# A two-layer decoder trunk on one core: residual stream kept feature-major, output projection with stationary weights, both norms folded

## The chip, the cores and the metric

The kernel runs on one core of a Trainium2 chip. The time is device microseconds of one execution. Before the change the median of three runs is 699.74 us (699.06 to 700.9).

## The reference, cut to what matters

512 prompt tokens and 8 × 4 = 32 sample tokens share the weights of two layers (D = 1024). All arrays are float32.

```python
def _rmsnorm(x, w):
    return x * lax.rsqrt(jnp.mean(x * x, axis=-1, keepdims=True) + EPS) * w

def _layer(x, ...):
    h = _rmsnorm(x, norm_w)
    z = h @ w_in                       # 1024 x 3584
    rq, rk, rv, rg, mq, mk, mv, mg, pu, pg = jnp.split(z, _split_points(), axis=-1)
    r_o = retention(rope(rq), rope(rk), rv)         # 6 heads x 64
    m_o = block_sparse_attention(rope(rmsnorm(mq)), rope(rmsnorm(mk)), mv)
    p_o = pooling(pu)                               # windows 2, 4, 8, 16
    mix = concat([r_o * silu(rg), m_o * silu(mg), p_o * silu(pg)])
    return x + mix @ w_out             # 1024 x 1024

for l in range(2):
    xp = _layer(xp, ...)   # 512 prompt tokens
    xs = _layer(xs, ...)   # 32 sample tokens, with caches and states
```

Besides the two results the new keys, values and states of both layers are outputs.

## The kernel before, in words

**Order.** Every piece of work is a generator that yields `R(engine, keys, get, mode)`: the engine (or a choice such as "ACT|DVE"), the flags it waits for, the buffers it takes, and the shape in which TensorE is used. `_Plan` (L118) takes the step that can start first by its modelled costs, so the program has one fixed order on each engine; at run time only semaphores delay it. SP issues the transfers, in its own fixed order: weight slices, cache pages, residual loads and stores share it.

**Projections.** A weight chunk ("mv", "mq", ..., "rg", "o0", "o1", "o2"; `order`, L422) is 384 or 256 columns wide and comes in four slices of two 128-row blocks each (`wraw`). ACT rounds a slice to fp32r and DVE (or POOL) subtracts to get the low part, both into `whl` (five buffers). A float32 product is three fp32r passes, hi·hi, lo·hi, hi·lo (`PASSES`), over 8 k-blocks: 24 matmuls for an output piece, which takes one of two PSUM banks "acc". In the token form (`tok_piece`, L474) 128 tokens of `XT` are the stationary operand and 384 or 256 weight columns stream: the trace calls it `acc<-whl,XT`, and its result is token-major. In the feature form (`feat_piece`, L483) 128 weight columns are stationary and the tokens stream, 256 of them for half 0 and 288 for half 1 (256 prompt and the 32 sample tokens): `acc<-XT,whl`, result feature-major. The gates and the pool input (pu, pg, mg, rg) have the feature form. The others, the output projection o0 to o2 among them, have the token form, and there the sample tokens go by a plain float32 product of their own (`sample_piece`, L506: `dec<-wraw,...`, 32 matmuls of half the chunk's width), joined by `join_sample`.

**Layer 0's norm** is folded: `xt` comes from the host feature-major, `split_tokens` multiplies by the norm's weights per feature (`ncol`) and splits into `XT`'s high and low part; `norm_tokens` and `split_sample` sum squares beside that, and `spread_norms` makes the token scales `rs`, and `Rb`, the same scales spread over all partitions. Projections' results are scaled afterwards: token-major ones by `rs` per partition, feature-major ones on DVE, `acc<-acc,Rb` (L1163, L1244).

**Output projection and layer 1's norm.** `split_mix` (L1491) writes the gated mix into `XT` once the last input chunk has been multiplied. `residual` (L1506) loads x in 15 pieces; `post_out` (L1521) adds them, token-major, into `mix` (`ytile`), and for the samples into a t1 buffer. After o2, `rmsnorm(l, t)` (L547) works for each of the four token tiles and the samples: ACT squares and sums, POOL takes the power −0.5, DVE multiplies by scale and weights (`SCALAR_TENSOR_TENSOR qT/kT<-mix,rst,pt`), TensorE transposes eight 128×128 blocks (`tr<-cst,qT`, L352), ACT and DVE write the high and low part into `XT`. In layer 1 the projections need no scale afterwards.

The lines that the steps of the prediction touch:

```python
    def tok_piece(ci, n, t, a, ks, i):
            mm(a[:, :W], XT[:, k, xl, t * 128:(t + 1) * 128], w1 if wl else w0, ...)
    def feat_piece(ci, n, f, half, a, ks, i):
        n0, n1 = (0, 256) if half == 0 else (256, NTOK)
            mm(a[:, :n1 - n0], wt[ci, k // 2][:, wl, c0:c0 + 128], XT[:, k, xl, n0:n1], ...)
```

Of the kernel before, what the change touches and what calls it, by code (L numbers as in the profile page):

```python
# [10 lines left out]
F32 = mybir.dt.float32  # L11
# [33 lines left out]
TOKENS = ["mq", "mv", "mk", "rq", "rv", "rk", "o0", "o1", "o2"]  # L45
# [68 lines left out]
SP_PRIO = 2  # L114
WARM = 1


class _Plan:  # L118
# [8 lines left out]
    SWITCH = 0.1  # L127

# [55 lines left out]
    def _start(self, t):  # L184
        engines, keys, get, mode = t["want"]
# [61 lines left out]
def R(engines, keys=(), get=(), mode=FULL):  # L247
    return engines, tuple(keys), tuple(get), mode
# [61 lines left out]
def trunk(ctx, tc, depth, xp, xt, xs, xst, kv, sret, spool, pt, nrow, ncol, lpar, w384, w256, cst, y0,  # L310
# [64 lines left out]
    def ytile(t, c0=0, W=D):  # L375

        return mix[:, c0 // 128:(c0 + W) // 128, t * 128:(t + 1) * 128]

    def col3(x):
        return x.rearrange("p (k c) -> p k c", c=128)  # L380

# [25 lines left out]
    ncolt = const.tile([128, 8], F32, name="ncol")  # L407
# [84 lines left out]
    def chunk(ci, outs, ks=KS_IN):  # L492

        for oi_, (piece, keys, post) in enumerate(outs):
            for i in range(0, 8, 2):
                s_ = ks[i] // 2
                yield R("PE", [("w", ci, s_)] + ([] if i else list(keys)), [] if i else ["acc"])
# [6 lines left out]
            X.spawn(post(a), 1, X.then())  # L504

    def sample_piece(ci, n, x, keys, post):  # L506
# [4 lines left out]
        yield R("PE", [("raw", ci, s_) for s_ in order_] + list(keys), ["dec"], COLS32)  # L511
# [35 lines left out]
    def rmsnorm(l, t, L):  # L547
        rows = 128 if t < 4 else NS
        tag = ("qT", "qT", "kT", "kT", "PT")[t]
        st = sb([128, 3], "rst", 4)  # L550
        if t == 4:
            yield R("SP", [("ys", l)], ["P", "P"])
            x = [buf("P")[:rows] for _ in range(2)]
            for half in range(2):
                S.dma_start(x[half], y0[SEQ:, :][:, half * 512:half * 512 + 512])
                X.flag("xs", l, at=X.dma(64))
            x = [col3(h) for h in x]
            yield R("ACT", [("xs", l)], [tag, tag])
            xn = [buf(tag)[:rows] for _ in range(2)]
            for half in range(2):  # L560
                A.activation(col3(xn[half]), x[half], AF.Square, accum_out=st[:rows, half:half + 1])
            yield R("POOL")
            G.tensor_tensor(out=st[:rows, 0:1], in0=st[:rows, 0:1], in1=st[:rows, 1:2], op=OP.add)
        else:
            x = ytile(t)
            pair = "xn", t // 2
            yield R("ACT", [("y", l, t)] + [("xn", l, t)] * (t % 2), [] if t % 2 else [tag])
            if t % 2 == 0:
                L[pair] = [buf(tag), 4]
                X.flag("xn", l, t + 1)  # L570
            xn = L[pair][0][:, t % 2 * D:(t % 2 + 1) * D]
            xn3 = col3(xn)
            A.activation(xn3, x, AF.Square, accum_out=st[:, 0:1])
            yield R("POOL")
            x, xn = [x[:, 0:4], x[:, 4:8]], [xn[:, 0:512], xn[:, 512:D]]
        rsq(st[:rows, 2:3], st[:rows, 0:1], 1, rows, 1.0 / D)
        c0 = t * 128

        def turned(half):
            yield R("PE", [("cst0",)], ["tr"], FULL if t < 4 else ROWS32)  # L580
            p = ps("tr")
            for i in range(4):
                tr(p[:, i * rows:(i + 1) * rows], xn[half][:, i * 128:(i + 1) * 128], rows)
            if t == 4:
                X.put(tag)
            else:
                L[pair][1] -= 1
                if not L[pair][1]:
                    X.put(tag)
            pv = p[:, :4 * rows].rearrange("p (k n) -> p k n", k=4)  # L590
            ksl = slice(half * 4, half * 4 + 4)
            yield R("ACT")
            A.copy(XT[:, ksl, 0, c0:c0 + rows], pv)
            if t == 4:
                A.copy(X32[:, ksl, :], pv)
            yield R("DVE")
            V.tensor_tensor(out=XT[:, ksl, 1, c0:c0 + rows], in0=pv,
                            in1=XT[:, ksl, 0, c0:c0 + rows].bitcast(F32), op=OP.subtract)
            X.put("tr")
            X.flag("x", l, t, half)  # L600

        for half in range(2):
            if half == 0 or t == 0:
                yield R("DVE", [("row", l, half)] + ([("row", l, 1)] if t else []))
            V.scalar_tensor_tensor(col3(xn[half]), x[half], st[:rows, 2:3], col3(L["row"][half][:rows]),
                                   op0=OP.mult, op1=OP.mult)
            if t == 4:
                X.put("P")
            X.spawn(turned(half), 0, X.then())
        if t == 4:  # L610
            X.flag("normed", l)

# [20 lines left out]
    def projected(a, dst, t, Ct, St, scale=None, eps=None, norm=None):  # L633
# [25 lines left out]
        if scale is None:  # L659
# [6 lines left out]
            def root():  # L666
                yield R("POOL")
                rsq(st[:rows, 1, :H], st[:rows, 0, :H], H, rows, 1.0 / HD, EPS if eps is None else eps)
                X.flag(*key)
# [132 lines left out]
    def layer(l):  # L802
# [3 lines left out]
        def parameters():  # L806
            yield R("SP", () if l else [("xs issued",)], ["pt"])
            rowp = L["rowp"] = buf("pt")
            if l:
                L["row"] = [rowp[:, :512], rowp[:, 512:D]]  # L810
                S.dma_start(rowp[:, :D], nrow[l:l + 1, :D].to_broadcast([128, D]))
                at = X.dma(512)
                for i in range(2):
                    X.flag("row", l, i, at=at)
                yield R("SP")
            S.dma_start(rowp[:, D:D + 256], nrow[l:l + 1, D:].to_broadcast([128, 256]))
# [3 lines left out]
            yield R("DVE", [("normed", l)] if l else ())  # L820
# [15 lines left out]
        def tables(i):  # L836
# [3 lines left out]
            for j, base in enumerate((cos, sin)):  # L840
                c0 = D + 128 * i + 64 * j
# [135 lines left out]
        def post_mq(t):  # L977
            def f(a):
                yield R("DVE", [("tabs", l, 0)], ["qk"])
                q_ = buf("qk")  # L980
                yield from projected(a, q_, t, L["tabs", 0][:, 0, t], L["tabs", 0][:, 1, t], eps=eps_of(t), norm=norm)
# [25 lines left out]
        def scaled_copy(out, a, t, keys=()):  # L1007

            if l:
                yield R("ACT|DVE", keys)  # L1010
                copy(out(), a)
                return
            yield R("ACT|DVE", [("rs", t // 2), *keys])
# [5 lines left out]
        norm = None if l else rs[:, 1, 4:5]  # L1019

        def eps_of(t):
            return None if l else rs[:128 if t < 4 else NS, 2, t:t + 1]

        def post_mv(t):
            def f(a):
# [4 lines left out]
                if t < 4:  # L1030
                    yield from scaled_copy(lambda: L["tv"][:, t], a[:, :384], t, [("tvb", l)])
# [862 lines left out]
```

## Time and profile before

| | |
|---|---|
| median of three runs | 699.74 us (699.06 to 700.9) |
| the profiled execution | 698.75 us |
| its span, first to last instruction | 697.0 us |
| mean granted clock of TensorE | 1.000 |
| transfers | 159.76 MB, 229 GB/s over the span |

The profile is of one execution. Its span leaves out 1.75 us of that execution's time, and the execution is 1.0 us below the median. Engines are PE (TensorE's products), PEld (its loads of the stationary operand, beside PE), DVE, ACT, POOL and SP (which issues transfers). A row such as `acc<-whl,XT` names what is written and what is read; the line of a row is that of a helper for nearly every operation (L342 products, L352 transposes, L304 everything else), so rows are told apart by their tiles.

### The profile page before, as it was taken

How to read it: one execution, taken by the hardware profiler on the slowest of the kernel's cores; microseconds unless marked ns; L12 is line 12 of the kernel's file. 1: busy time of each engine (PE TensorE's matmuls, PEld its weight loads, DVE VectorE, ACT ScalarE, POOL GpSimd, SP SyncE). 2: the span in 40 equal slices, each digit the busy share in tenths (PEclk: the TensorE clock that was granted, in tenths of full speed). 3: DMA queues.
4: the chain of work that ended last, by engine and by line, in shares of the span. 5: the costliest groups of instructions: out<-in, count | busy, mean ns of one | idle time of the engine just before them, and what ended most of it. 6: DMA issues, size and time to landing. Idle time of an engine off the chain costs nothing.

```text
span 697.0 us, 16955 instructions
## 1 busy us (share of the span) xinstructions
PE 676.4 (97%) x5940; PEld 568.5 (82%) x5940; DVE 489.4 (70%) x1169; ACT 330.6 (47%) x831; POOL 106.8 (15%) x134
## 2 busy tenths in 40 slices
PE   7999999999999999899989999999999999999998
PEld 6997777777788879889978778777687888999998
DVE  6789988785662668975494699775845556877642
ACT  7453765662342334464363437676724234256520
POOL 4332223000000022200021223230100000151000
PEclk9999999999999999999999999999999999999999
DMA  8667978898989886435653887998899996020552
GB/s 314 226 205 231 287 232 274 258 310 291 325 261 296 304 266 210 119 124 174 192 177 129 265 270 246 303 314 288 291 278 293 336 321 227 2 83 20 173 176 79
DMA packets 111366, 159.76 MB, mean 229 GB/s; under 512 B 13937, under 2 KB 96114, under 8 KB 111282
## 3 DMA queue, kind: packets, MB, share of 16 engines
q1 hardware_dynamic: 111010, 158.43, 69.8%
q8 instruction: 47, 0.77, 0.4%
q10 hardware_dynamic: 272, 0.26, 0.2%
q14 instruction: 37, 0.30, 0.1%
HBM read 148.80 MB, written 9.84 MB: 228 GB/s over the span
## 4 chain that ended last, share of the span: by engine, by line
PE 86%; DVE 8%; ACT 2%; issue 2%; DMA 1%; POOL 0%; DVEq 0%; ACTq 0%
PE acc L342 54%; PE pv L342 12%; PE dec L342 10%; PE tr L352 6%; PE att L342 4%; DVE whl L304 2%; DVE XT L304 1%; DMA mix<-xt 1%; ACT whl L304 1%; DVE t L304 1%; DVE acc L304 1%; DVE qk L304 0%; ACT kT L304 0%; DVE kT L304 0%; DMA pk<-kv 0%
## 5 line engine op out<-in xcount | busy, mean ns | idle before, releaser
L342 PE MATMUL acc<-whl,XT 128*128 128x384 f32 (+1 forms) x1680 | 312.6, 338 | 4.7 <-ACT whl L304 3.2
L342 PEld LDWEIGHTS acc<-whl,XT 128*128 128x128 f32 x1680 | 282.2, 190 | 23.8 <-issue 14.0
L342 PE MATMUL acc<-XT,whl 128*128 128x256 f32 (+1 forms) x960 | 139.6, 295 | 4.0 <-DVE t L304 2.4
L342 PEld LDWEIGHTS acc<-XT,whl 128*128 128x128 f32 x960 | 124.7, 189 | 15.0 <-issue 10.4
L304 ACT CAST whl<-wraw 128x768 fp32r<-128x768 f32 (+1 forms) x100 | 77.0, 781 | 48.8 <-PE acc L342 42.8
L304 DVE TENSOR_TENSOR whl<-wraw,whl 128x768 fp32r<-128x768 f32 (+1 forms) x91 | 83.3, 928 | 16.6 <-ACT whl L304 16.0
L342 PE MATMUL dec<-pk,qblk 128*32 128x256 f32 x768 | 48.3, 383 | 0.0
L304 DVE TENSOR_TENSOR pv<-pv,cst 128x384 f32<-128x384 f32 x40 | 22.5, 563 | 28.3 <-PE pv L342 27.8
L342 PEld LDWEIGHTS dec<-pk,qblk 128*32 128x32 f32 x768 | 21.8, 109 | 17.4 <-issue 4.3
L304 DVE TENSOR_TENSOR mix<-acc,qk 128x384 f32<-128x384 f32 (+1 forms) x24 | 12.2, 508 | 24.7 <-PE acc L342 23.8
L304 ACT ACTIVATE P<-att,ast 128x128 f32<-128x128 f32 (+3 forms) x48 | 25.2, 530 | 8.4 <-DVE ast L304 8.2
L304 POOL TENSOR_TENSOR qst<-qst,mhalf 128x6 f32<-128x6 f32 (+1 forms) x20 | 26.5, 1324 | 1.7
L304 POOL TENSOR_TENSOR whl<-wraw,whl 128x768 fp32r<-128x768 f32 (+1 forms) x9 | 17.7, 1971 | 53.7 <-issue 28.5
L304 DVE TENSOR_REDUCE stat<-dec 128x1 f32<-128x256 f32 x32 | 13.5, 421 | 15.4 <-PE dec L342 15.1
L304 ACT ACTIVATE dPT<-dec 128x256 f32<-128x256 f32 x32 | 12.2, 382 | 24.8 <-PE pv L342 24.7
L304 POOL TENSOR_TENSOR gst<-gst,reps 128x6 f32<-128x6 f32 x4 | 0.8, 200 | 150.2 <-DVE gst L304 150.2
L304 ACT ACTIVATE dP<-dec,stat 128x256 f32<-128x256 f32 x32 | 15.1, 473 | 15.8 <-DVE stat L304 15.7
L304 ACT COPY PT<-tr 128x128 f32<-128x128 f32 (+3 forms) x40 | 16.0, 429 | 12.6 <-PE tr L352 12.6
L304 ACT ACTIVATE t<-acc 128x256 f32<-128x256 f32 (+1 forms) x32 | 12.6, 394 | 18.9 <-PE acc L342 10.2
L304 DVE TENSOR_REDUCE ast<-att 128x2 f32<-128x256 f32 (+3 forms) x24 | 19.8, 825 | 0.8
L352 PE MATMUL tr<-cst,P 128*128 128x128 f32 x120 | 19.3, 278 | 0.8 <-DVE so L304 0.6
L304 ACT ACTIVATE PT<-PT,gst 128x64 f32<-128x64 f32 x48 | 16.8, 428 | 6.6 <-POOL gst L304 6.6
(504 smaller groups left out, 1184.8 us busy)
## 6 DMA issues: line engine op xcount, KB each, us to landing
pk<-kv SPq DMA_DIRECT2D x256, 192.0 KB, 3.8
wraw<-w SPq DMA_DIRECT2D x76, 384.0 KB, 4.9
wraw<-w SPq DMA_DIRECT2D x24, 256.0 KB, 4.5
y<-mix SPq DMA_DIRECT2D x4, 512.0 KB, 3.6
mix<-xt SPq DMA_DIRECT2D x7, 256.0 KB, 5.9
pk<-w SPq DMA_DIRECT2D x4, 384.0 KB, 4.9
o_vp<-tv SPq DMA_DIRECT2D x8, 192.0 KB, 2.7
o_kp<-qk SPq DMA_DIRECT2D x8, 192.0 KB, 3.8
```

Of the source, the lines that this page charges most:

```text
L304: return f(*args, **kw)
L342: nc.tensor.matmul(out, lhsT, rhs, start=start, stop=stop)
L352: nc.tensor.transpose(out, in_, ident[:n, :n])
```

## The change

The output projection takes the feature form in both layers, sample tokens included (as columns 256 to 287 of half 1), so the residual stream is feature-major throughout: `mix` holds x + mix @ w_out by features, `xsT` that of the samples, and `y0`, the results and the residual loads have feature-major layouts (16 pieces of 128 KB a layer). `rmsnorm` with its transposes is gone; layer 1 uses layer 0's `split_tokens`, `norm_tokens`, `split_sample` and `spread_norms`, so all its projections are scaled afterwards. The first chunk, mv, goes by halves of the tokens in both layers: half 0 in the "att" banks and half 1 in the "acc" banks, and its bank is copied out before it is scaled. `norm_tokens` squares on ACT and adds on DVE alone. The planner gets two constants for changes of TensorE's shape (STAY, LEAVE).

```diff
-TOKENS = ["mq", "mv", "mk", "rq", "rv", "rk", "o0", "o1", "o2"]
+TOKENS = ["mq", "mv", "mk", "rq", "rv", "rk"]
...
                 if mode != self.mode:
-                    late = self.HOLD if self.mode == FULL else 0.3
+                    late = (hold or self.HOLD) if self.mode == FULL else 0.3
+                elif mode != FULL:
+                    late = self.STAY
                 c = max(at + late, self.free[e])
+            elif e == "PE" and self.mode != FULL:
+                c = s + self.LEAVE
...
-    def rmsnorm(l, t, L):
...
-            x = ytile(t)
...
-            A.activation(xn3, x, AF.Square, accum_out=st[:, 0:1])
...
-                tr(p[:, i * rows:(i + 1) * rows], xn[half][:, i * 128:(i + 1) * 128], rows)
...
         def post_mv(t):
...
-                    yield from scaled_copy(lambda: L["tv"][:, t], a[:, :384], t, [("tvb", l)])
-                    X.put("acc" if l or t < 2 else "att")
+                    yield R("ACT|DVE", [("tvb", l)])
+                    copy(L["tv"][:, t], a[:, :384])
+                    X.put("att" if t < 2 else "acc")
+                    yield from scaled_copy(lambda: L["tv"][:, t], L["tv"][:, t], t)
...
             def f(a):
-                if l == 0:
-                    yield R("DVE", [("Rb",)])
-                    V.tensor_tensor(out=a[:, :n], in0=a[:, :n], in1=Rb[:, n0:n1], op=OP.mult)
+                yield R("DVE", [("Rb", l)])
+                V.tensor_tensor(out=a[:, :n], in0=a[:, :n], in1=Rb[:, n0:n1], op=OP.mult)
...
+        def split_mixs():
+            yield R("ACT|DVE", [("dec", l, g) for g in range(2)] + [("inputs", l, 1)] +
+                    [(n, l, f, 1) for n, m in (("pg", 2), ("rg", 3)) for f in range(m)])
+            copy(XT[:, :, 0, SEQ:], mixs)
+            yield R("DVE")
+            V.tensor_tensor(out=XT[:, :, 1, SEQ:], in0=mixs, in1=XT[:, :, 0, SEQ:].bitcast(F32), op=OP.subtract)
+            X.flag("mixs", l)
...
+        def post_out(h, f):
+            def g(a):
+                yield R("DVE", [("res", l, h, f)])
+                out = mix[:, f, 256 * h:256 * h + 256]
+                V.tensor_tensor(out=out, in0=a[:, :256], in1=L["res", h, f][:, :256], op=OP.add)
+                if h:
+                    V.tensor_tensor(out=xsT[:, f], in0=a[:, 256:256 + NS], in1=xsT[:, f], op=OP.add)
+                X.put("acc")
                 X.put("qk")
...
+                X.flag("xt", l + 1, h, f)
+                send((y0 if l < depth - 1 else o_yp)[h, f // 2][:, f % 2 * 256:f % 2 * 256 + 256], out, 128)
...
             for n in ("o0", "o1", "o2"):
-                yield from tokens(n, lambda t: post_out(n, t), lambda t: [("mix", l, t)], KS_OUT)
+                steps = chunk(c(n), [(feat(n, f, h), mixed(h), post_out(h, fo)) for h, f, fo in out_pieces(n)], KS_OUT, 0)
+                for i, x in enumerate(steps):
+                    yield x
+                    if n == "o2" and i in (7, 15):
+                        X.flag("oh", l, i // 8)
...
-    def split_tokens(h, kp):
+    def split_tokens(l, h, kp):
...
-        yield R("ACT|DVE", [("xt", h, kp), ("ncol",)])
+        yield R("ACT|DVE", [("xt", l, h, k) for k in ks] + ([("oh", l - 1, h)] if l else [("ncol",)]))
...
-    def norm_tokens(h):
...
-            yield R("ACT|POOL", [("xt", h, 2 * i), ("xt", h, 2 * i + 1)], [] if i else [tag])
...
+        for k0, k1 in ((0, 3), (3, 6), (6, 8)):
+            yield R("ACT", [("xt", l, h, k) for k in range(k0, k1)], [] if k0 else [tag])
```

Two places of the order show what moves. The first is PE between the layers: the end of o2 and the beginning of layer 1's mv (`tr<-cst,qT/kT/PT` are the transposes of rmsnorm, `dec<-wraw,X_71` a float32 product of the sample tokens). Before:

```order
L352 MATMUL tr<-cst,qT 128x128 x4
L342 MATMUL acc<-whl,XT 128x256 x6
L352 MATMUL tr<-cst,qT 128x128 x4
L342 MATMUL acc<-whl,XT 128x256 x24
L352 MATMUL tr<-cst,qT 128x128 x4
L342 MATMUL acc<-whl,XT 128x256 x6
L352 MATMUL tr<-cst,qT 128x128 x4
L342 MATMUL acc<-whl,XT 128x384 x6
L352 MATMUL tr<-cst,PT 128x32 x8
L352 MATMUL tr<-cst,kT 128x128 x8
L342 MATMUL dec<-wraw,X_71 32x192 x16
L342 MATMUL acc<-whl,XT 128x384 x6
```

With the change:

```order
L351 MATMUL acc<-XT,whl 128x256 x48
L351 MATMUL acc<-XT,whl 128x288 x48
L351 MATMUL att<-whl,XT 128x384 x48
L351 MATMUL acc<-whl,XT 128x384 x12
L351 MATMUL tr<-ones,ssum 32x1 x4
L351 MATMUL tr<-ones,qT 128x1 x2
L351 MATMUL acc<-whl,XT 128x384 x12
L351 MATMUL dec<-wraw,X_71 32x192 x16
L351 MATMUL tr<-ones,kT 128x1 x2
L351 MATMUL acc<-whl,XT 128x384 x24
L351 MATMUL tr<-P,ones 128x128 x4
L351 MATMUL tr<-ssum,ones 128x32
```

The 40 transposes are gone, half 0 of mv stands right behind o2, and the small products of the folded norm stand inside mv's half 1 and after it.

The second place is DVE at the same boundary, where post_out's additions (`mix<-acc,qk`), the splits into `XT` and the low parts of mv's weight slices (`whl`) share one queue. Before:

```order
L304 TENSOR_TENSOR mix<-acc,qk 128x2x128
L304 SCALAR_TENSOR_TENSOR qT<-mix,rst,pt 128x512 x2
L304 TENSOR_TENSOR mix<-acc,qk 128x2x128
L304 TENSOR_TENSOR XT<-tr,XT 128x4x128
L304 SCALAR_TENSOR_TENSOR qT<-mix,rst,pt 128x512 x2
L304 TENSOR_TENSOR XT<-tr,XT 128x4x128
L304 TENSOR_TENSOR mix<-acc,qk 128x2x128
L304 SCALAR_TENSOR_TENSOR PT<-P,rst,pt 32x512 x2
L304 TENSOR_TENSOR XT<-tr,XT 128x4x128
L304 TENSOR_TENSOR mix<-acc,qk 128x2x128
```

With the change:

```order
L313 TENSOR_TENSOR mix<-acc,qk 128x256
L313 TENSOR_SCALAR XT<-mix,ncol 128x256 x2
L313 SCALAR_TENSOR_TENSOR XT<-mix,ncol,XT 128x256 x6
L313 TENSOR_TENSOR mix<-acc,qk 128x256
L313 TENSOR_TENSOR xsT<-acc,xsT 128x32
L313 SCALAR_TENSOR_TENSOR XT<-mix,ncol,XT 128x256 x2
L313 TENSOR_TENSOR whl<-wraw,whl 128x768 x2
L313 TENSOR_TENSOR mix<-acc,qk 128x256
L313 TENSOR_TENSOR xsT<-acc,xsT 128x32
L313 TENSOR_SCALAR XT<-mix,ncol 128x256 x2
L313 SCALAR_TENSOR_TENSOR XT<-mix,ncol,XT 128x256 x8
L313 TENSOR_TENSOR X_71<-xsT,ncol 128x256
```

The splits of half 0 now stand between the additions of o2's two halves, and eight of them, the additions of half 1's two pieces and two weight slices come before those of half 1.

## Rows read from the trace of the kernel before

**Rows 1.** The page: busy time by engine, and the chain that ended last.

```profile
PE 676.4 (97%) x5940; PEld 568.5 (82%) x5940; DVE 489.4 (70%) x1169; ACT 330.6 (47%) x831; POOL 106.8 (15%) x134
...
PE 86%; DVE 8%; ACT 2%; issue 2%; DMA 1%; POOL 0%; DVEq 0%; ACTq 0%
```

**Rows 2.** Timeline of PE, end of layer 1: start us, us, operation, idle before.

```profile
654.50 1.51 PE L342 MATMUL dec<-wraw,mixs 128*32 128x192 f32 x32
...
663.05 11.73 PE L342 MATMUL acc<-whl,XT 128*128 128x384 f32 x66
674.71 1.08 PE L342 MATMUL dec<-wraw,mixs 128*32 128x128 f32 x32
```

**Rows 3.** Timeline of PE, between the layers.

```profile
346.09 0.60 PE L352 MATMUL tr<-cst,qT 128*128 128x128 f32 x4
...
347.59 2.99 PE L342 MATMUL acc<-whl,XT 128*128 128x256 f32 x24
350.42 0.60 PE L352 MATMUL tr<-cst,qT 128*128 128x128 f32 x4
...
354.13 0.43 PE L352 MATMUL tr<-cst,PT 32*128 32x32 f32 x4 [0.50 <-DVE XT L304]
355.75 1.09 PE L352 MATMUL tr<-cst,kT 128*128 128x128 f32 x8 [1.20 <-DVE XT L304]
...
360.44 1.25 PE L352 MATMUL tr<-cst,kT 128*128 128x128 f32 x8 [0.90 <-DVE XT L304]
361.45 4.81 PE L342 MATMUL acc<-whl,XT 128*128 128x384 f32 x26
```

**Rows 4.** Timeline of PE, two stretches of the feature form.

```profile
509.26 5.92 PE L342 MATMUL acc<-XT,whl 128*128 128x256 f32 x48
...
630.97 7.31 PE L342 MATMUL acc<-XT,whl 128*128 128x256 f32 x54
```

**Rows 5.** Timeline of PE, layer 0's folded norm.

```profile
24.38 0.24 PE L342 MATMUL tr<-ones,ssum 128*32 128x1 f32 x8
...
26.77 0.50 PE L342 MATMUL tr<-ones,qT 128*128 128x1 f32 x4
...
28.64 0.61 PE L342 MATMUL tr<-ones,kT 128*128 128x1 f32 x4
...
35.26 1.05 PE L342 MATMUL tr<-P,ones 128*128 128x128 f32 x8
36.24 0.40 PE L342 MATMUL tr<-ssum,ones 32*128 32x32 f32 x2
```

**Rows 6.** Waits of PE, whole span: total us, times, longest.

```profile
PE acc L342 <- ACT whl L304: 3.2, 1, 3.2
...
PE acc L342 <- DVE t L304: 2.4, 2, 1.8
...
PE acc L342 <- DVE mix L304: 1.3, 1, 1.3
...
PE dec L342 <- DVE mixs L304: 0.8, 1, 0.8
```

**Rows 7.** DVE's groups by form, whole span: count, busy us, mean ns.

```profile
L304 DVE TENSOR_TENSOR acc<-acc,Rb 128x288 f32<-128x288 f32 x8 | 3.7, 458 | 0.0
```

**Rows 8.** Timeline of DVE, at the start and between the layers.

```profile
16.20 3.25 DVE L304 SCALAR_TENSOR_TENSOR XT<-mix,ncol,XT 128x256 fp32r<-128x256 f32 x8
...
354.00 1.39 DVE L304 SCALAR_TENSOR_TENSOR kT<-mix,rst,pt 128x512 f32<-128x512 f32 x2
...
355.93 0.95 DVE L304 TENSOR_TENSOR whl<-wraw,whl 128x768 fp32r<-128x768 f32 x1
356.80 2.98 DVE L304 SCALAR_TENSOR_TENSOR kT<-mix,rst,pt 128x512 f32<-128x512 f32 x2
```

**Rows 9.** Timeline of POOL, between the layers.

```profile
356.05 2.52 POOL L304 TENSOR_TENSOR whl<-wraw,whl 128x768 fp32r<-128x768 f32 x1
```

**Rows 10.** Timeline of DVE, the end.

```profile
693.80 0.42 DVE L304 TENSOR_TENSOR mix<-acc,qk 128x256 f32<-128x256 f32 x1 [2.48 <-PE acc L342]
```

More of the change, by code (lines that the diff above doesn't have):

```diff
@@ L184, in _start @@
     def _start(self, t):
-        engines, keys, get, mode = t["want"]
+        engines, keys, get, mode, hold = t["want"]
         at = t["ready"]
@@ L1007, in scaled_copy @@
         def scaled_copy(out, a, t, keys=()):
[L1009 to L1013, printed above, removed]
+            yield R("ACT|DVE", [("rs", l, t // 2), *keys])
             if X.engine == "ACT":
@@ L1617, in dense @@
-            X.spawn(residual(), 2)
-            yield from rg()
+            for h in range(2):
+                for kp in range(4):
+                    yield R("PE", [("w", ci, kp), ("xk", l, h, kp)], [] if kp else ["acc" if h else "att"] * 2)
+                    if kp == 0:
+                        a = [ps("acc") for _ in range(2)] if h else [x[:, j] for j, x in enumerate([ps("att")] * 2)]
+                    for j in range(2):
+                        for k in (2 * kp, 2 * kp + 1):
+                            tok_piece(ci, "mv", 2 * h + j, a[j], KS_IN, k)
+                    if h:
+                        X.put("whl")
+                for j in range(2):
+                    X.spawn(post_mv(2 * h + j)(a[j]), 1, X.then())
@@ new lines, in dense @@
+            inputs = order[1:10]
+            for n in inputs:
+                if n == "pu":
+                    X.spawn(start_pool(), 2)
+                if n == inputs[-1]:
+                    for t in range(4):
+                        X.spawn(split_mix(t), 3)
+                    X.spawn(split_mixs(), 3)
+                    X.spawn(residual(), 2)
+                steps = tokens(n, {"mq": post_mq, "mk": post_mk, "rq": post_rq, "rv": post_rv,
+                                   "rk": post_rk}[n]) if n in TOKENS else features(n)
+                for i, x in enumerate(steps):
+                    yield x
+                    if n == inputs[-1] and i in (11, 23):
+                        X.flag("inputs", l, i // 12)
@@ L1698, in norm_tokens @@
+        X.flag("xk", l, h, kp)
+    def norm_tokens(l, h):
         cs = slice(256 * h, 256 * h + 256)
         tag = ("qT", "kT")[h]
-        for i in range(2):
-            yield R("ACT|POOL", [("xt", h, 2 * i), ("xt", h, 2 * i + 1)], [] if i else [tag])
-            if i == 0:
+        for k0, k1 in ((0, 3), (3, 6), (6, 8)):
+            yield R("ACT", [("xt", l, h, k) for k in range(k0, k1)], [] if k0 else [tag])
+            if k0 == 0:
                 sq = buf(tag)[:, :2048].rearrange("p (k n) -> p k n", k=8)
-            x = mix[:, 4 * i:4 * i + 4, cs]
-            if X.engine == "ACT":
-                A.activation(sq[:, 4 * i:4 * i + 4], x, AF.Square)
-            else:
-                G.tensor_tensor(out=sq[:, 4 * i:4 * i + 4], in0=x, in1=x, op=OP.mult)
@@ L1709, in norm_tokens @@
-        yield R("DVE|POOL")
-        add2(sq[:, 0:4], sq[:, 0:4], sq[:, 4:8], OP.add)
-        yield R("DVE|POOL")
-        add2(sq[:, 0:2], sq[:, 0:2], sq[:, 2:4], OP.add)
-        yield R("DVE|POOL")
-        add2(sq[:, 0], sq[:, 0], sq[:, 1], OP.add)
+            A.activation(sq[:, k0:k1], mix[:, k0:k1, cs], AF.Square)
+            if k0 == 3:
+                yield R("DVE")
+                add2(sq[:, 0:3], sq[:, 0:3], sq[:, 3:6], OP.add)
+                for k in (1, 2):
+                    yield R("DVE")
+                    add2(sq[:, 0], sq[:, 0], sq[:, k], OP.add)
@@ L1715, in norm_tokens @@
+        for k in (6, 7):
+            yield R("DVE")
+            add2(sq[:, 0], sq[:, 0], sq[:, k], OP.add)
         yield R("PE", [("zeros",)], ["tr"])
```

347 lines of the change are left out of this document (108 added, 239 removed).

## Prediction

> **What bounds the kernel now.** I read the page first: busy time by engine and the chain that ended last [rows 1]. PE is busy in 676.4 of 697.0 us and 86% of the chain lies on it, so time is gained where PE gets less to do or waits less. Then I read PE's timeline, which gives the price of each kind of product: the 384-wide one takes (674.71 − 663.05) / 66 = 0.177 us, the 256-wide one of the token form (350.42 − 347.59) / 24 = 0.118 us [rows 2, 3]. These go with the streamed columns, so which operand is stationary matters little. In the feature form 48 matmuls of 256 columns took 5.92 us, 0.123 each with the run's end in it [rows 4]. In the second stretch of that group 54 matmuls took 7.31 us; by the program's order six of them are 256 wide and the rest 288, so a 288-wide one costs at most (7.31 − 6 × 0.118) / 48 = 0.138, and by columns 0.118 × 288 / 256 = 0.133. Last I read PE's waits [rows 6], of which no one is over 3.2 us, and the boundary between the layers [rows 3].
>
> **The change part by part** (us, against the profiled 698.75).
>
> Output products. A layer has 192 products of 384 columns and 96 of 256 now: 192 × 0.177 + 96 × 0.118 = 45.3. Afterwards it has 384 of the feature form, half of each width: 192 × (0.118 + 0.133) = 48.2, with the upper prices 192 × (0.123 + 0.138) = 50.1. That is +2.9 a layer, **+5.9** in all, at most +9.7. I take the lower prices, because the upper ones contain a run's end, which long dense runs have once.
> By the Trainium skill ("TensorE: Matmul & The Clock Gate", sections "LDWEIGHTS (loading the stationary operand)" and "Back-to-back issue gap") a load costs its columns at 1.2 per ns, about 107 ns for 128 by estimate, and the spacing of matmuls is set by load and product together. The change has 96 more loads a layer, so 192 × 107 ns would be some 20 us more if loads lay in the open; the 0.118 of the 256-wide rows speaks against that, as it is barely over one such load.
>
> Sample products. Per layer three go, 1.51 twice and 1.08 [rows 2]: 4.1, in both layers **−8.2**. Their additions (join_sample) go too, off PE's path. The samples now cost the 32 extra columns, counted above.
>
> The boundary. The stretch from the first transpose (346.09) to the last one's successor (361.45) takes 15.36 [rows 3]. What stays of it are 36 products of o2 at 0.118, 12 of mv at 0.177 and the sample product of mv, 1.5 as [rows 2]: 7.9. So **−7.5**: some 4 of it transposes, 0.50 + 1.20 + 0.90 = 2.6 waits for DVE's XT, the rest the changes from one kind to another.
>
> Layer 1's folded norm on PE. The same five groups as in layer 0: 0.24 + 0.50 + 0.61 + 1.05 + 0.40 [rows 5], **+2.8**. The squares go to ACT (47% busy [rows 1]), the additions to DVE; nobody on PE waits for them before the token scales are needed.
>
> Gates of layer 1. Each of 16 pieces gets a multiply of 0.46 on DVE [rows 7] ahead of its tanh, and gives its bank back that much later. Layer 0, which does this already, has two waits for `t`, 2.4 in all [rows 6], and layer 1 none. I take half of it, **+1.2** (0 to 2.4), since only one of two places recurs where DVE's queue is the same.
>
> New waits at the boundary. Half 0 of `XT` can be split as soon as o2's half 0 is multiplied; mv then starts after o2's half 1, 48 × 0.133 = 6.4 later. In that time DVE's queue holds eight subtractions of 0.41 (3.25 / 8 [rows 8]), two roundings (bounded by the same 0.41), two additions of 0.42 [rows 10], the sample addition, at most as long, and two weight slices of 0.95 [rows 8]: 3.3 + 0.8 + 0.8 + 0.4 + 1.9 = 7.2 against 6.4. But mv needs the last k-blocks only 36 × 0.177 = 6.4 after its first, and the first subtractions come first. Half 1 has the 48 × 0.177 = 8.5 of mv's half 0 as cover, with eight subtractions and two roundings, 4.1, in front. mv's half 0 goes to the "att" banks, so post_out's last additions, which free "acc", hold up nobody. I take one wait of today's size, **+0.5** [rows 3], between 0 and the 2.6 + 1.6 of the second rival.
>
> Starts of the output products. PE waits there 1.3 for `mix` and 0.8 for `mixs` [rows 6]. The flags are finer now (per group of k-blocks), and the samples are needed only in half 1, 72 × 0.118 = 8.5 after o0's start. On the other side the high and low parts of the samples are new on ACT and DVE, and a piece lasts 24 × 0.118 = 2.8 instead of 4.2, so DVE has less time per piece. **0**, between −2.1 and +2.1.
>
> Weights and residuals. A chunk's slices come free during its last piece, 3.2 long instead of 4.2, as they do today after the gates' chunks; there PE waits for no slice (its only wait for `whl` is the start's 3.2 [rows 6]), so 0. The residual loads are 16 for 15, all issued well ahead, three buffers deep; SP's queue loses the sample stores and gets 16 stores a layer where layer 0 had 4 and 3. Weights for the next layer stand behind them. A slice asked for a few tenths later is covered by the slices in hand: 0, and if that cover were gone, a wait as at the start.
>
> The end. After the last product DVE adds the residual in 0.42 [rows 10] and now the samples' too, and one store more follows: **+0.4**, at most twice 0.42.
>
> **Sum.** 5.9 − 8.2 − 7.5 + 2.8 + 1.2 + 0.5 + 0 + 0.4 = −4.9: 693.8 for the profiled execution. The median stands 1.0 above that one, so **694.8**.
>
> **The rivals.** What a measurement of this kernel can tell from no change is about 0.3%, 2.1 us: 697.6 to 701.8.
>
> *The waits vanish.* If the finer flags end the waits at the output products (−2.1), no gate of layer 1 waits (−1.2) and the boundary is dense (−0.5), it gives 694.8 − 3.8 = **691.0**. For it speaks that each of these waits is short, so that a little slack ends it; against it that DVE is 70% busy [rows 1] and gets more to do.
>
> *The boundary gives back.* Today's waits for XT, 2.6 [rows 3], may come back, since the splits follow additions that follow o2's products just as the transposes did. And POOL takes one of mv's weight slices beside them: in the trace a pair of DVE operations with two inputs in SBUF took 1.39 alone and 2.98 beside POOL's slice of 2.52 [rows 8, 9], 1.6 more. It stands in POOL's order at the boundary again. Together 4.2 in place of 0.5: **698.5**, about the same as before. For it: DVE's queue was 7.2 against 6.4 above. Against it: mv's k-blocks are needed one after the other, and 1.6 lands on PE only if all the slack is gone.
> The Trainium skill ("SBUF — State Buffer", section "SBUF: two separate sides") says that the port pair shared by the two engines is held for a whole instruction, also against a DVE operation with two SBUF inputs; the pair's 2.98 beside 2.52 agrees with it.
>
> *Slower: DVE becomes the gate of the banks in layer 1.* There are two "acc" banks. A gate's bank is free after the multiply, the tanh and the product with it, three times about 0.46 [rows 7], 1.4, and a feature piece lasts 24 × 0.118 = 2.8 or 24 × 0.133 = 3.2. DVE may therefore come 1.4 late before PE waits. If its queue (attention, sample blocks and weight slices are in it) is later than that at half of the 16 pieces, each costs what the two waits of layer 0 cost on the mean, 1.2: 8 × 1.2 − 1.2 = 8.4 more, **703.2**. Against it: layer 0 has the same pieces and only two such waits.
>
> *The feature form is dearer in a long run than its columns say* (loads of the stationary operand showing between streams). The rows leave at most 0.123 + 0.138 for a pair against 0.251, 3.8 in all, **698.6**; it joins the second rival in its place.
>
> **How the numbers follow.** The forecast, with a range of its own of 692.5 to 697.6 (the unknowns of the single terms), has a chance of 0.55; the vanishing waits 0.20; the boundary or the dearer products, around 699, 0.16; the slower one 0.09. Faster by over 0.3% is the first two less the upper edge of the forecast: 0.70. Within 0.3% is that edge and the third: 0.21. Slower is the last: 0.09. The range leaves out the slower rival and little else: from 691.0 less two, since the start's POOL square is gone as well, **689.0**, to 698.6 with the upper prices of the smaller waits on top (1.2 for the gates, 1.5 for the output's starts), **701.5**.
>
> **What would show it.** Right: no `tr<-cst,qT` or `tr<-cst,kT` of rmsnorm between the layers, and from o2's last product to mv's end hardly an idle stretch over 0.5; output runs of `acc<-XT,whl` at 0.118 to 0.123 and 0.133 to 0.138 a product, about 48 a layer; no `dec<-wraw,mixs`; PE's busy time down by some 4. Wrong: PE waits for `XT` between the layers of over 2.5 in all, waits for `t` of over 2.4 in layer 1's gates, waits for `whl` or `qk` inside the output products, or a matmul pitch above 0.14 there. A time under 691 would mean that waits which I left standing were gone, over 699 that one of the rivals decides.

## The result, and the profile after

The changed kernel takes 707.42 us in the median (705.82 to 709.98), the kernel before, measured beside it, 700.03 (699.06 to 700.9): a ratio of 1.0117 with a 95% interval of 1.010 to 1.0134. It is slower by 7.4 us where 4.9 less were forecast. The profiled execution took 705.82 us with a span of 704.0, 7.0 more than the span before.

The page of the changed kernel, busy time by engine and the chain that ended last:

```profile
PE 676.5 (96%) x5926; PEld 573.9 (82%) x5926; DVE 497.0 (71%) x1211; ACT 337.6 (48%) x843; POOL 103.3 (15%) x130
...
PE 81%; DVE 14%; issue 2%; ACT 1%; DMA 1%; POOL 0%; SPq 0%; DVEq 0%; ACTq 0%; POOLq 0%
```

Against [rows 1] DVE's share of the chain has risen from 8% to 14%, and PE's has fallen from 86% to 81%, while PE's busy time is the same. So the reader has to look for two things: work that PE lost, and something that made the remaining work longer or later.

The work that was to go has gone. PE's timeline of the changed kernel, behind the last product of o2 in layer 0 and at the end of layer 1 (start us, us, operation):

```profile
351.79 8.59 PE L351 MATMUL att<-whl,XT 128*128 128x384 f32 x48
360.22 2.26 PE L351 MATMUL acc<-whl,XT 128*128 128x384 f32 x12
362.41 0.24 PE L351 MATMUL tr<-ones,ssum 128*32 128x1 f32 x8
362.59 0.61 PE L351 MATMUL tr<-ones,qT 128*128 128x1 f32 x4
...
366.77 0.61 PE L351 MATMUL tr<-ones,kT 128*128 128x1 f32 x4
...
371.54 1.05 PE L351 MATMUL tr<-P,ones 128*128 128x128 f32 x8
372.52 0.40 PE L351 MATMUL tr<-ssum,ones 32*128 32x32 f32 x2
372.85 1.68 PE L351 MATMUL acc<-whl,XT 128*128 128x384 f32 x8
...
663.69 36.51 PE L351 MATMUL acc<-XT,whl 128*128 128x288 f32 x288
```

There are no transposes and no waits where [rows 3] had both. The folded norm's five groups take 2.9 us. The last row is one dense run of 288 products of the feature form, by the program's order 120 of 256 columns and 168 of 288: 120 × 0.118 + 168 × 0.133 = 36.5, the measured 36.51.

The waits have grown instead. PE's waits over the whole span (total us, times, longest), which answer to [rows 6]:

```profile
PE tr L361 <- DVE row L313: 4.3, 2, 3.4
PE acc L351 <- DVE whl L313: 4.1, 6, 1.3
...
PE tr L361 <- DVE qk L313: 2.5, 2, 1.6
PE acc L351 <- DVE qk L313: 2.4, 2, 1.6
...
PE acc L351 <- DVE t L313: 0.9, 2, 0.6
```

All rows of that view add up to 16.8 us before and to 23.6 after, 6.8 more. Two of them are new and large: `row`, and `whl` behind DVE. PE's timeline in layer 1's rg and at the start of o0 shows where most of them lie (idle time ahead and what ended it in brackets):

```profile
635.01 1.05 PE L351 MATMUL acc<-XT,whl 128*128 128x288 f32 x6
639.42 0.27 PE L361 MATMUL tr<-cst,row 128*64 128x128 f32 x1 [3.37 <-DVE row L313]
640.33 0.27 PE L361 MATMUL tr<-cst,row 128*64 128x128 f32 x1 [0.64 <-DVE mixs L313]
641.22 6.21 PE L351 MATMUL acc<-XT,whl 128*128 128x288 f32 x36 [0.62 <-DVE t L313]
...
648.60 0.50 PE L351 MATMUL pv<-tv,kst 96*128 96x512 f32 x1 [0.92 <-DVE pt L313]
...
650.68 0.94 PE L351 MATMUL acc<-XT,whl 128*128 128x256 f32 x4 [1.34 <-DVE whl L313]
...
652.86 5.70 PE L351 MATMUL acc<-XT,whl 128*128 128x256 f32 x40 [0.23 <-DVE whl L313]
```

DVE's timeline in the same place says why:

```profile
637.22 0.69 DVE L313 TENSOR_TENSOR On<-On,comb 128x512 f32<-128x512 f32 x1
637.95 1.01 DVE L313 TENSOR_REDUCE row<-On 128x64 f32<-128x512 f32 x1
...
640.22 0.47 DVE L313 TENSOR_TENSOR acc<-acc,Rb 128x288 f32<-128x288 f32 x1
```

`On<-On,comb` belongs to the last step of the sample attention (`combine`), which weighs the results of eight cached blocks, sums them into `row` and has `row` transposed by PE. In the kernel before, this instruction of layer 1 stood at 595 us, long ahead of rg:

```profile
595.26 0.69 DVE L304 TENSOR_TENSOR On<-On,comb 128x512 f32<-128x512 f32 x1
```

With the change it stands at 637 us, in the middle of rg's gates. PE's second gate piece ended at 636.06 (635.01 + 1.05), and its multiply by `Rb` started at 640.22, 4.2 us later, because the combine is ahead of it in DVE's queue; and PE, in its own fixed order, stands in front of the transposes of `row`.

Then the clock. The windows view of the changed kernel (start and end, length, busy time of PE, PEld, DVE, ACT, POOL, granted clock, DMA share, GB/s):

```profile
303.00:306.00 3.00, 3.00 (x13) 2.72 (x13) 2.82 (x8) 1.81 (x4) 0.00 (x0) 0.50 0.88 243
...
636.00:640.79 4.79, 0.60 (x3) 0.22 (x2) 4.40 (x15) 0.48 (x2) 0.77 (x2) 1.00 0.00 0
640.79:644.20 3.41, 2.98 (x12) 2.98 (x13) 2.84 (x10) 1.47 (x4) 0.00 (x0) 0.50 0.01 2
...
651.03:654.44 3.41, 3.17 (x14) 2.71 (x13) 3.35 (x6) 2.76 (x5) 0.00 (x0) 0.50 0.50 149
```

Three times TensorE was granted the lower of its two levels, 1.2 GHz, in the products behind a group of waits. In its profiled execution the kernel before shows no such stretch inside its work. The price: 36 products took 6.21 us where 4.87 were measured at the higher level (run e8 below), 40 of 256 columns 5.70 instead of 40 × 0.118 = 4.7, and at 303 us 18 of them took 3.73 instead of 2.1. Together 1.3 + 1.0 + 1.6 = 3.9 us. They lie in PE's busy time, which is the same before and after (676.4 and 676.5) only because the work itself fell by 3.8.

The third place is the start of o0 in layer 0, PE's timeline of the changed kernel:

```profile
299.75 0.97 PE L351 MATMUL acc<-XT,whl 128*128 128x256 f32 x6 [0.59 <-DVE whl L313]
302.03 0.74 PE L351 MATMUL acc<-XT,whl 128*128 128x256 f32 x4 [1.31 <-DVE whl L313]
...
303.29 3.73 PE L351 MATMUL acc<-XT,whl 128*128 128x256 f32 x18
```

### The profile page after: what moved, and what is told of

Same layout as the page of the kernel before. It is cut to its first block, busy times and chain, and to the rows that moved or that the text cites. A ratio compares the mean times of both kernels' runs of the same rounds, so it can differ in the third digit from the quotient of the medians.

```text
span 704.0 us, 16987 instructions
## 1 busy us (share of the span) xinstructions
PE 676.5 (96%) x5926; PEld 573.9 (82%) x5926; DVE 497.0 (71%) x1211; ACT 337.6 (48%) x843; POOL 103.3 (15%) x130
## 4 chain that ended last, share of the span: by engine, by line
PE 81%; DVE 14%; issue 2%; ACT 1%; DMA 1%; POOL 0%; SPq 0%; DVEq 0%; ACTq 0%; POOLq 0%
PE acc L351 50%; PE pv L351 10%; PE dec L351 9%; PE att L351 6%; PE tr L361 5%; DVE whl L313 2%; DVE qk L313 1%; DVE t L313 1%; DVE acc L313 1%; DVE qT L313 1%; DVE row L313 1%; DVE mix L313 1%; DVE XT L313 1%; DVE P L313 1%; DMA mix<-xt 1%
## 5 line engine op out<-in xcount | busy, mean ns | idle before, releaser
L351 PE MATMUL acc<-XT,whl 128*128 128x256 f32 (+1 forms) x1728 | 244.7, 296 | 7.1 <-DVE whl L313 3.9
L351 PEld LDWEIGHTS acc<-XT,whl 128*128 128x128 f32 x1728 | 227.2, 192 | 17.9 <-issue 6.6
L351 PE MATMUL acc<-whl,XT 128*128 128x384 f32 x1056 | 206.0, 344 | 0.2 <-DVE whl L313 0.2
L351 PEld LDWEIGHTS acc<-whl,XT 128*128 128x128 f32 x1056 | 181.2, 188 | 13.4 <-issue 9.9
L313 DVE TENSOR_TENSOR mix<-acc,qk 128x256 f32<-128x256 f32 x32 | 13.5, 423 | 39.1 <-PE acc L351 38.9
L351 PE MATMUL att<-whl,XT 128*128 128x384 f32 x96 | 20.4, 376 | 3.1 <-ACT whl L313 3.1
L351 PEld LDWEIGHTS att<-whl,XT 128*128 128x128 f32 x96 | 19.4, 216 | 4.7 <-ACT whl L313 4.2
L313 DVE TENSOR_TENSOR t<-acc,cst 128x192 f32<-128x192 f32 x32 | 10.0, 353 | 18.7 <-PE acc L351 18.6
L313 POOL TENSOR_TENSOR whl<-wraw,whl 128x768 fp32r<-128x768 f32 (+1 forms) x8 | 13.5, 1695 | 63.7 <-ACT whl L313 63.3
L361 PE MATMUL tr<-cst,qk 128*128 128x128 f32 (+1 forms) x108 | 17.6, 272 | 3.6 <-DVE qk L313 2.5
```

The source lines that it names most:

```text
L313: return f(*args, **kw)
L351: nc.tensor.matmul(out, lhsT, rhs, start=start, stop=stop)
L361: nc.tensor.transpose(out, in_, ident[:n, :n])
```

## The experiments

Theory A: the loss lies in the order of DVE's work at two places (the combine in front of rg's gates, the weight slices at o0's start) and in the clock behind these waits. Rivals: B, the multiply of the folded norm is too much for DVE wherever the combine stands; C, the planner's two new constants spoiled the order. Each run is compared with runs of the kernel before on the same chip; ratios are to that kernel, and the changed kernel's own is 1.0117.

**e1.** The combine's second half waits for rg's second gate.

```diff
-            yield R("DVE")
+            yield R("DVE", [("freed", "rg", l, 1, 1)] if l and g else [])
             V.tensor_tensor(out=c_[:, 3, :], in0=c_[:, 2, :], in1=st[:, 1, :], op=OP.mult)
...
                 X.put("acc")
+                X.flag("freed", *done)
                 yield R("DVE|POOL", keys)
```

> The changed kernel in all but one place: in layer 1 the second half of the last combine step of the sample attention (eight DVE instructions, from the product with the sums to the row's sum) waits until the second gate piece of rg's half 1 has given its bank back. Nothing is computed otherwise. Theory A (these DVE instructions stand before the two multiplies that free the acc banks, so PE runs dry there, its clock falls, and the weight splits behind are late): the waits of 3.37, 0.64 and 0.62 us at 636 to 641 us and most of those for whl at 648 to 653 go, 700 to 703 us. Theory B (the multiply of the folded norm in layer 1's gates is itself too much for DVE, wherever the combine stands): 706 to 708 us, the waits only move. Theory C (the planner's two new constants made the order worse): 706 to 708 us.

Measured: 701.28 us, 1.0031 (1.0013 to 1.0048). Six of the 7.4 us are back, which theory B does not allow. Up to 636 us PE, DVE, ACT and POOL run the same instructions in the same order as in the changed kernel; behind that the planner laid more anew than the eight DVE instructions: rounding of weight slices stands earlier on ACT and one low part has gone to POOL, so the run does not part the wait in rg from those at o0's start. PE's timeline of e1 in rg shows that a wait is left, now for the gate's own product:

```profile
639.58 1.07 PE L351 MATMUL acc<-XT,whl 128*128 128x288 f32 x6 [1.99 <-DVE t L313]
```

**e2.** No multiply in layer 1's rg.

```diff
-                yield R("DVE", [("Rb", l)])
-                V.tensor_tensor(out=a[:, :n], in0=a[:, :n], in1=Rb[:, n0:n1], op=OP.mult)
+                if l == 0 or done[0] != "rg":
+                    yield R("DVE", [("Rb", l)])
+                    V.tensor_tensor(out=a[:, :n], in0=a[:, :n], in1=Rb[:, n0:n1], op=OP.mult)
```

> The changed kernel without the multiply by Rb in layer 1's rg gates alone (so these six gate pieces are left unscaled); everything before rg is in the same order. Theory A: the combine still stands before the products that free the two banks, which come at about 639.5 us instead of 641.2, so only 1 to 2.5 us are won: 704.5 to 706.5 us, a wait of over 2 us stays. Theory B: the wait goes and 5 us or more are won, 702 us or less.

Measured: 704.04 us, 1.0084 (1.0068 to 1.0101), half a microsecond better than theory A's range and not theory B's 702. The wait stays. The longest of PE's waits in e2:

```profile
PE tr L361 <- DVE row L313: 4.5, 2, 3.6
```

**e3.** The planner's rules of before.

```diff
-                elif mode != FULL:
-                    late = self.STAY
...
-            elif e == "PE" and self.mode != FULL:
-                c = s + self.LEAVE
```

> The changed kernel with the planner's rules of before (STAY and LEAVE taken out). Theory C: the sample units move up and 5 us or more are won, 702 us or less. Theory A: by the order the last units of the sample attention still lie in layer 1's rk and rg, and the combine still stands before the multiplies of rg's half 1, so PE waits there again: 703 to 708 us.

Measured: 703.11 us, 1.0055 (1.0037 to 1.0072). This is inside A's range and short of C's 702, but 4 us better than the change, about half of the loss. A's number came, its reason only in part: the combine still stands in rg, at 636 us, and PE waits there again, but only 1.8 and for `t`. The wait for `row` is gone from layer 1 (0.9 in layer 0 is the only one), since PE's order has put its transposes later; at o0's start PE waits 0.6 for `whl` and 1.3 for `mix`. So the constants have a share, since any other order lays the waits elsewhere, and this run does not refute theory C.

**e4.** Sample units first.

```diff
-                            X.spawn(unit(g, n), 2)
+                            X.spawn(unit(g, n), 0)
```

> The changed kernel with the sample attention's units at priority 0 instead of 2, so that the last one lies at the start of layer 1's rg instead of past its middle, and the combine before the gates' multiplies of half 0. Theory A: no wait of PE over 1.5 us in rg's half 1 and fewer for whl behind it: 699 to 702 us. Theory B: waits for the gates' banks stay spread over rg, 705 us or more. Theory C: 705 us or more.

Measured: 706.13 us, 1.0116 (1.0098 to 1.0133). Theory A's forecast of the time failed. Its forecast for the place held: rg's half 1 has no wait, and PE's waits for `row` fell to 1.1 in all. But others came, elsewhere. PE's waits in e4:

```profile
PE acc L351 <- DVE whl L313: 3.2, 5, 1.7
PE acc L351 <- DVE mix L313: 3.1, 1, 3.1
...
PE tr L361 <- DVE P L313: 2.0, 1, 2.0
```

The theory was narrowed by this: not the late sample attention as such costs, but where DVE's long steps fall. This run alone does not show it; the next ones test it.

**e5.** The first two pieces of o0 together, into the att banks.

```diff
+                if n == "o0":
+                    for i in range(0, 8, 2):
+                        yield R("PE", [("w", c(n), KS_OUT[i] // 2)] + mixed(0)(i), [] if i else ["att"] * 2)
...
+                        for j in range(2):
+                            for i_ in (i, i + 1):
+                                feat(n, pieces[j][1], 0)(a2[:, j], KS_OUT, i_)
```

> The changed kernel, but the first two pieces of o0 are multiplied together, slice by slice, into the two att banks, so that each weight slice lasts 12 products of 256 columns (1.42 us) instead of 6 (0.71 us); DVE's low part of a slice takes 0.95 us. Theory A2 (at the start of the output products PE uses up slices faster than DVE splits them, since the first pieces are now 256 wide instead of 384, and the clock falls after these waits): waits for whl at 299 to 301 and at 648 to 653 us and the stretches of clock 0.50 behind them go in both layers, while the wait of 3.4 us in rg stays: 3 to 6 us less, 701.5 to 704.5 us. Theory B2 (the slices are late because of the stall in rg before, or because of ACT): layer 0 gains nothing, 706 to 708 us.

Measured: 702.44 us, 1.0052 (1.0032 to 1.0072). PE's timeline of e5 in layer 0, where three rows stood above:

```profile
295.46 6.21 PE L351 MATMUL att<-XT,whl 128*128 128x256 f32 x48
```

No wait and no lower clock here. Rival B2 falls, since layer 0 gained with the work ahead of o0 in the same order: o0 lasts 21.0 us there, to the first product of o1, and 23.9 in the changed kernel. DVE's timeline of the changed kernel in layer 0 shows what the slices waited for:

```profile
297.04 0.96 DVE L313 TENSOR_TENSOR whl<-wraw,whl 128x768 fp32r<-128x768 f32 x1 [0.27 <-ACT whl L313]
...
298.74 0.95 DVE L313 TENSOR_TENSOR whl<-wraw,whl 128x768 fp32r<-128x768 f32 x1
...
301.03 1.81 DVE L313 TENSOR_TENSOR whl<-wraw,whl 128x768 fp32r<-128x768 f32 x2
```

PE used a slice up in 0.71 us. DVE needs 0.95 for its low part, and with the last steps of the gates between them it began the slices 1.7 and 2.3 us apart. In layer 1 the forecast came only in part: the lower clock at 651 us went, but a wait for `whl` of 1.5 is left, where the changed kernel had 1.34 + 0.23. PE's timeline of e5 in layer 1:

```profile
646.99 1.47 PE L351 MATMUL att<-XT,whl 128*128 128x256 f32 x10 [1.51 <-DVE whl L313]
```

**e6.** Both edits, e1's and e5's.

> Both edits, the two pieces of o0 together and the combine's second half behind rg's second gate of half 1. If the loss of the change is the sum of the two places: 8 to 10 us less than the changed kernel, 697 to 699.5 us, no clock below 1.00 at 300 us and at 640 to 655 us. If one wait only moves to the next place: 700 to 703 us.

Measured: 699.54 us, 1.0001 (0.9988 to 1.0015). The whole loss is gone, though 697 to 699.5 was just missed, and the gain that was forecast has not come. In the profiled execution the clock is 1.000 (0.995 to 0.998 in the nine others). Its span is 8.6 us shorter than the changed kernel's; 5.8 of them are PE's busy time, with the clock's 3.9 in it, and 2.8 its idle time. The waits of 2.0 us for `t` and of 2.1 for `whl` are left in rg and at o0's start, and those for `qk` in layer 1's mk and pu.

**e7.** e6 with the planner's rules of before.

> Both edits, and the planner's rules of before. If these constants matter little once the two places are mended: within 1.5 us of the run before it, 696.5 to 700 us. If they spread the waits otherwise: 701 us or more.

Measured: 701.41 us, 1.0027 (1.0014 to 1.004), just inside the second forecast; one wait of 4.1 us, for `row`, now stands inside o0's first pieces, and the clock falls behind it.

**e8.** The stall filled.

```diff
+                    if n == inputs[-1] and l and i == 20:
+                        fill = ps("att")
+                        for j in range(24):
+                            nc.tensor.matmul(fill[:, 0, :288], wt[c(n), 0][:, 0, :128], XT[:, 0, 0, 256:NTOK],
+                                             start=j == 0, stop=j == 23)
```

> The changed kernel with 24 products of 288 columns, whose result nobody reads, put on PE into the stall in front of rg's last piece of layer 1; the order of all else on PE stays. Theory D (besides the wait, the lower clock behind it costs): the idle 3.4 us are filled by 3.2 us of products, the clock stays 1.00 from 640 to 645 us and the 36 products behind it take 4.8 us instead of 6.2, 1.4 us less up to the end of rg; of the whole 0.5 to 1.5 us less, 705.5 to 707 us. Theory E (the lower clock has nothing to do with the idle time ahead): it falls at 640 us all the same.

Measured: 707.22 us, 1.0115 (1.0096 to 1.0134). PE's timeline of e8:

```profile
632.62 3.36 PE L1521 MATMUL att<-XT,whl 128*128 128x288 f32 x24
636.20 0.27 PE L361 MATMUL tr<-cst,row 128*64 128x128 f32 x1 [0.22 <-DVE row L313]
...
638.00 4.87 PE L351 MATMUL acc<-XT,whl 128*128 128x288 f32 x36 [0.62 <-DVE t L313]
...
646.73 0.73 PE L351 MATMUL acc<-XT,whl 128*128 128x256 f32 x4 [1.59 <-DVE whl L313]
...
648.91 7.64 PE L351 MATMUL acc<-XT,whl 128*128 128x256 f32 x40 [0.69 <-DVE whl L313]
```

Theory D holds for the place: with the idle time filled the 36 products take 4.87 us, not 6.21. It does not for the whole: the lower clock came at 648 us instead, behind the next waits, and 40 products took 7.64 us. Nothing was won.

**e9, e10.** If order decides, another order should do. Two other sets of the planner's constants were run, each together with both edits. The constants of e10 (those of e9 stand in its forecast):

```diff
-SP_PRIO = 2
+SP_PRIO = 3
...
-    MARGIN = 0.4
+    MARGIN = 0.3
-    HOLD = 0.6
+    HOLD = 0.8
-    STAY = 0.2
-    LEAVE = 0.2
-    POOL_LAST = 3.0
+    STAY = 0.4
+    LEAVE = 0.4
+    POOL_LAST = 2.0
...
-                            X.spawn(unit(g, n), 2)
+                            X.spawn(unit(g, n), 3)
```

> The kernel of both edits (two pieces of o0 together, the combine's second half behind rg's gates, here behind its first gate of half 1) with other constants in the planner: sample units at priority 1, sample pieces at 3, STAY 0.1, LEAVE 0. Nothing else is computed. If what is left of the forecast gain lies in waits of PE on DVE (1.6, 1.0 and 1.6 us at 398 to 429 us, 2.0 and 2.1 at 632 to 641) and in the clock behind them, an order with fewer of them is faster than the kernel before: 694 to 698 us. If the waits only move: 698.5 to 702 us.

Measured: 694.48 us, 0.992 (0.9893 to 0.9947), inside the first forecast.

> The same with a third set of constants: units at priority 3, sample pieces at 3, HOLD 0.8, MARGIN 0.3, STAY and LEAVE 0.4, POOL_LAST 2.0, the combine behind rg's second gate. Waits fewer: 694 to 698 us; waits moved: 698.5 to 702 us.

Measured: 691.49 us, 0.9889 (0.9871 to 0.9908), better than was expected, and the fastest version of this study: 8 us less than the kernel before, 16 less than the change as it was made.

**e11, e12.** The same constants without the two edits, on the changed kernel and on the kernel before.

> The changed kernel with the planner's constants of the run before (units and sample pieces at priority 3, HOLD 0.8, MARGIN 0.3, STAY and LEAVE 0.4, POOL_LAST 2.0) and neither of the two edits. If the two edits carry the gain of that run (8 us over the edits' sum was won by constants, 5 and 6 by the edits alone): 696 to 700 us, with waits for whl at o0's start back. If the order alone carries it: 691 to 693 us.

Measured: 692.23 us, 0.9911 (0.9883 to 0.9939). The constants alone carry it; beside them the two edits add nothing that these intervals could tell. PE's waits in e11:

```profile
PE tr L361 <- DVE row L313: 5.8, 2, 3.0
...
PE acc L351 <- POOL whl L313: 0.5, 2, 0.2
...
PE acc L351 <- DVE whl L313: 0.2, 1, 0.2
```

The waits for `whl` behind DVE fell from 4.1 to 0.2 us, and now two of 0.2 us are for POOL's slices, since POOL makes one at o0's start in either layer. The wait for `row` has not gone: it stands in rg of both layers now, 2.8 and 3.0 us, with the clock at 0.50 behind each. That is the second correction to theory A: not each of its two places has to be mended. Nor are the waits the whole gain. The page of e11, whose span is 691.0 us:

```profile
PE 669.6 (97%) x5926; PEld 571.0 (83%) x5926; DVE 493.7 (71%) x1206; ACT 335.5 (49%) x843; POOL 110.4 (16%) x135
```

Against the changed kernel's profiled execution PE's idle time fell by 6.1 us (27.5 to 21.4) and its busy time by 6.9 (676.5 to 669.6). What of the 6.9 is the clock, and what the new order of the different kinds of products, was not separated.

> The kernel before the change with the same constants. If they are simply better constants for any order: 692 to 696 us. If an order is only good for the kernel that it was found for: 699 us or more; the last sample units lie in rg here too, so waits as in the changed kernel are possible and 703 to 708 us would not surprise.

Measured: 713.49 us, 1.0211 (1.0185 to 1.0237). The same constants (with the rules for STAY and LEAVE put in, which it lacked) make the kernel before slower by 14 us. PE's waits in e12:

```profile
PE acc L349 <- DVE t L311: 5.5, 3, 3.7
PE tr L359 <- DVE row L311: 3.8, 2, 2.8
```

So the gain of e10 and e11 is not one of better constants as such. What stays open: no constants were picked for the kernel before, whose best order may lie below 699 us too; and why the planner, after the change, lays layer 1's sample units later was not traced to one step.

## Why the prediction was wrong

**Right: the work on PE.** Output products: +5.9 forecast; 192 × (0.118 + 0.133) holds in the dense run of 288 products to 0.01 us. The 20 us that the prediction estimated from the Trainium skill ("TensorE: Matmul & The Clock Gate", section "LDWEIGHTS (loading the stationary operand)"), if loads lay in the open, did not come: that run has none of them. Sample products: −8.2, their rows are gone. The folded norm's products: +2.8 forecast, 2.9 measured. The boundary: mv, from its first product to that of mq, took 25.98 us before (351.92 to 377.90) and takes 21.06 (351.79 to 372.85); four transposes inside o2 went as well (4 × 0.35), and one sample product of 1.5 us now lies behind mv's end. Net −4.9 − 1.4 + 1.5 = −4.8 with the fold in it, against −7.5 + 2.8 + 0.5 = −4.2. PE's busy time without the clock's 3.9 fell by 3.8, where some 4 was forecast. The second rival (the boundary gives back) did not come true, nor did the dearer products. Two slips in the prediction's sums change nothing: the output products' terms give 2 × 2.9 = 5.8, not 5.9, and the upper bound's 698.6 + 1.2 + 1.5 give 701.3, not 701.5. The measured 707.4 lies beyond that bound, and beyond the slower rival's 703.2.

**Wrong, first: "Weights and residuals ... so 0".** The step argued that the gates' chunks have no wait for `whl` today. But at an output chunk's start DVE has more to do than slices: the last steps of the gates, and in layer 1 splits of the mix and sums of `pt`, stand between them. In layer 0 the slices began 1.7 and 2.3 us apart. PE uses up the first chunk's slices at 0.71 us each instead of 1.06 (6 × 0.177). It waited 3.5 us for them at the two starts (0.59 + 1.31 and 1.34 + 0.23), of 4.1 in all. e5 shows this for layer 0, where a slower use of the slices ended the waits; in layer 1 it did not. The term "Starts of the output products" lost its 2.1 of waits for `mix` and `mixs` only to get these.

**Wrong, second: "Gates of layer 1 ... +1.2 (0 to 2.4)".** The price of a gate was taken from layer 0, "where DVE's queue is the same". It is not: 4.6 us of waits (3.37 + 0.64 + 0.62) came from a combine in the same queue. The slower rival named DVE's lateness at the gates, and the point of decision, 1.4 us, was passed (4.2 us late); but it spread the price over eight pieces, and e2 shows that the multiply is the smaller part. The prediction's sign for it, waits for `t` of over 2.4 in layer 1's gates, did not appear (0.6): DVE's lateness shows as waits for `row` and `mixs`.

**Wrong, third, and left out: the rest of the order.** The sum was made as if everything away from the edited lines stayed where it was. The combine moved by 42 us, and PE's waits for `qk` grew from 1.1 + 0.8 to 2.5 + 2.4. A list scheduler works all of this out anew after any edit. In numbers: the forecast had the waits down by 0.9 (−2.6 at the boundary, +1.2, +0.5), and they went up by 6.8; it had nothing for the clock, which cost 3.9. −4.9 + 7.7 + 3.9 = +6.7, and the span grew by 7.0. That is a sum for the profiled executions, and it closes; which wait comes from which step of the new order was shown for the two places of theory A alone.

With another order the change gives 692.2 us (e11), where 694.8 was forecast. This does not make the forecast right: it was for the order that was there to be read.

## What to carry to other kernels

Where a scheduler makes a fixed order, an edit has two effects, the work it removes and a new order, and here the planner's constants alone, which change nothing that is computed, moved the changed kernel between 692 and 707 us and the kernel before between 699 and 713, while the work removed was worth some 4. So look through the whole new order for long steps on a busy engine that now stand ahead of a buffer's release, wherever they are, before adding up terms; and try the change with several sets of the scheduler's constants before it is judged. When a piece becomes narrower, set the time in which it uses up one weight slice against the time in which the splitting engine makes one, with all else that this engine has to do there.

## What had not been expected of the hardware

The granted clock fell to 0.50, the 1.2 GHz level, behind groups of waits of PE of 1.9 us (0.59 + 1.31) to 4.6 in all. That is a second price of a wait, 1.0 to 1.6 us for each stretch here. Neither the length of a wait nor the order told it. The kernel before had one of 1.3 us at o0's start in layer 0, with the clock at 1.00 behind it, as its timeline of PE and its windows show:

```profile
303.56 1.31 PE L342 MATMUL acc<-whl,XT 128*128 128x384 f32 x6 [1.30 <-DVE mix L304]
```

```profile
304.00:308.00 4.00, 4.00 (x47) 3.17 (x46) 2.40 (x6) 1.55 (x3) 0.00 (x0) 1.00 0.29 68
```

The changed kernel had 0.59 and 1.31 in the same place, and there it fell. e6 had waits of 2.0 and 2.1 us in layer 1, and its clock stayed at 1.00. In e1 it fell at 434 us, behind waits of 1.03 and 1.64 us; the changed kernel has the same instructions in the same order there, with waits of 1.04 and 1.64, and its clock stayed at 1.00. The windows of e1, and then of the changed kernel:

```profile
435.00:440.00 5.00, 5.00 (x34) 4.98 (x34) 1.93 (x7) 2.24 (x8) 1.08 (x1) 0.78 0.83 270
```

```profile
435.00:440.00 5.00, 5.00 (x43) 5.00 (x41) 3.24 (x12) 2.66 (x9) 1.60 (x2) 1.00 0.98 315
```

So the same work can meet the lower clock in one execution and not in another. Filling one stall moved the fall to the next (e8). The changed kernel's executions also spread more: 705.82 to 709.98 us against 699.06 to 700.9 for the kernel before. In the runs the spread goes with the clock: the changed kernel's two executions at a mean clock of 0.989 and 0.991 took 706.0 and 705.8, the two at 0.986 took 708.9 and 710.0; of e1's ten, the four at 0.998 took 699.4 to 700.4 and the six at 0.990 to 0.994 took 701.0 to 703.8. What sets a fall off was not found.
